# A hybrid diffusion block on one core: shift and scale of four K tiles as VectorE products, low halves of the sweep weights on GpSimd

## The chip, the cores and the metric

The kernel runs on one core of a Trainium2 chip. The metric is the device time of one execution in microseconds. The core has a matrix engine (TensorE, PE in the profile), a vector engine (VectorE, DVE), a scalar engine (ScalarE, ACT), GpSimd (POOL) and SyncE (SP), which in this kernel only issues transfers. A page of the profile gives times in us unless it marks them ns.

## The reference

The reference is one layer over 256 latent tokens and 256 context tokens, each with 2048 channels. Only the latent stream is returned. What matters for this change is the beginning:

```
sh1, sc1, g1, sh2, sc2, g2       = split(silu(c)     @ w_ada + b_ada, 6)    # latent tokens
sh1c, sc1c, ...                  = split(silu(c_ctx) @ w_ada + b_ada, 6)    # context tokens
h_l = rms_norm(x,   norm1_w) * (1 + sc1)  + sh1
h_c = rms_norm(ctx, norm1_w) * (1 + sc1c) + sh1c
projections = h_l @ w_in, h_c @ w_in
```

So each of the 2048 channels needs a shift and a scale for the latent stream and another pair for the context stream. Each of these is a dot product of 2048 terms: a column of `w_ada` with silu(c) or with silu(c_ctx). After that come gated linear attention, differential attention, gates, output projections, and a gated feed-forward network with a convolution. They use the other four sixths of the conditioning (`g1, sh2, sc2, g2`), for the latent stream alone. All inputs are 32-bit floats.

## The kernel before

Activations are kept transposed: 16 tiles, one for each group of 128 channels (the K tiles), channels on the partitions, tokens along the free dimension. Products are taken in a rounded 32-bit format. Every operand is split in two for accuracy: a high half, a rounded copy made by ScalarE (`split`, line 206), and a low half, the difference, made by VectorE (line 213). Three products of halves replace one exact product. `hl`/`ll` and `hc`/`lc` are the high and low halves of the modulated latent and context tokens.

**The first stage** is the `with` block from line 363 to line 599. It normalises and modulates both streams and at the same time multiplies them with a first part of `w_in`, the sweep weights: 896 columns, accumulated over the 16 K tiles in seven PSUM banks. In the loop of line 580, one turn k multiplies tile k (`sweep_row` for the first 512 columns, four token groups; `sweep_col` for the other 384 columns, three groups) and prepares tile k + 1. Preparing a tile means:

- `ada_rows` (line 463): sixteen small matrix products with silu(c) and silu(c_ctx) as the stationary side (columns 0 and 1 of `ccol_s`, 32 columns each) and the conditioning weights `w_ad1` of this tile as the moving side, 256 columns, in full 32-bit precision, in four row groups of the bank `ab`. ScalarE copies the result to `row`.
- `ada_cols` (line 474): two transposes on TensorE bring the sums onto the partitions. VectorE adds the four groups (`both`, line 482) and makes scale and shift (`shsc`, lines 483 and 484).
- `stage` (line 487): VectorE multiplies x by scale and by the root `z` (line 496), ScalarE adds the shift and rounds to the high half (line 498), VectorE makes the low half (line 502); once for each stream.
- `sweep_splits` (line 507): the halves of the sweep weights of the tile, 512 and 384 columns wide.

The first two tiles are prepared ahead of the loop, among the sums of squares for the norms.

**The order.** Inside this stage nearly everything is pinned: `pinned`, `kept` and `ordered_dma` hold each engine to the order in which the lines are written. SP issues the transfers in that order, too: the two inputs, tiles 0 and 1, then in each turn (`load`, line 406) the sweep weights and the four quarters of `w_ad1` of tile k + 2. A tile of conditioning weights is 2 MB, four buffers of 4 KB per partition; there are `SLOTS` = 12 such buffers, and four buffers for sweep weights. Outside this stage, the order is chosen by a planner with its own estimate of durations and by priorities written in the code.

**The other conditioning** is done on VectorE, in all the stages after this one. `w_ada` lies transposed in memory, so that output channels are on the partitions, and `cb` holds silu(c) broadcast to all partitions. `ada_load` (line 347) loads half a row tile, 512 KB, and `ada_dot` (line 354) multiplies it by half of `cb` and sums it, in one instruction. There are 128 of these; `ada_next(n)` (line 673) is called with fractions that say how many become due at each point. Six of them are done early, in turns 4 to 9 of the first stage (`EARLY_ADA`).

Of the kernel before, what the change touches and what calls it, by code (L numbers as in the profile page):

```python
# [9 lines left out]
F32 = mybir.dt.float32  # L10
# [3 lines left out]
AF = mybir.ActivationFunctionType  # L14
# [4 lines left out]
P = 128  # L19
# [19 lines left out]
SWW = 32 + C0 + (NGK + 1) * P  # L39
UPS = 6  # L40
CONVS = 7
SLOTS = 12
EARLY_ADA = 4, 10
GATE_ADA = [0.25] * 4 + [0.5] * 16 + [1] * 12
NRM = [(0, 0)] * 2 + [(j, j + 1) for j in range(12)] + [(12, 14), (14, 16)]

# [28 lines left out]
def _lay_out(i):  # L75
# [3 lines left out]
    w_ada = np.asarray(i["w_ada"])[0]  # L79
    w_in = np.asarray(i["w_in"])[0]  # L80
    a["xl"], a["xc"] = [np.ascontiguousarray(v.T.reshape(KT, P, T).transpose(1, 0, 2)) for v in (x, ctx)]
    c2 = np.stack([np.asarray(i["c"])[0], np.asarray(i["c_ctx"])])
    a["ccol"] = np.ascontiguousarray(c2.reshape(2, KT, P).transpose(2, 1, 0))
    g1 = w_ada[:, :2 * D].reshape(KT, P, 2, KT, P)
    a["w_ad1"] = np.ascontiguousarray(g1.transpose(3, 1, 0, 2, 4).reshape(KT, P, 2 * D))
    a["w_ada"] = np.ascontiguousarray(w_ada[:, 2 * D:].T.reshape(64, P, D))
    sweep = list(range(GA, GA + 32)) + list(range(GV, GV + C0)) + list(range(GK, GK + NGK * P)) + list(range(DKO, DKO + P))
# [59 lines left out]
def layer_kernel(tc, I, out):  # L147
# [3 lines left out]
    with es:  # L151
# [46 lines left out]
            for step in [work.pop(0) for _ in range(len(work))]:  # L198
                step()

        def split(raw, n, lows=None):


            hi = st.tile([P, 512], F32R, tag="hi", bufs=4, name="whi")
            lo = st.tile([P, 512], F32R, tag="lo", bufs=4, name="wlo")
            copied[0] = S.copy(hi[:, :n], raw)  # L206
            if pin[0]:
                tc.keep_in_program_order(copied[0])
            splits[0] += 1
            e = G if splits[1] and splits[0] % splits[1] == 0 else V  # L210

            def low():
                i = e.tensor_tensor(lo[:, :n], raw, hi[:, :n].bitcast(F32), op=ALU.subtract)  # L213
                if pin[0]:
                    tc.keep_in_program_order(i)
                if e is V:
                    copied[1] = i

            if lows is None:
                low()  # L220
            else:
                lows.append(low)
            return hi, lo

        def fetch(src, n):
            raw = st.tile([P, 1024], F32, tag="raw", bufs=4, name="wraw")
            nc.sync.dma_start(raw[:, :n], src)
            return raw
# [6 lines left out]
        ENDED = "h0 l0 h1 l1 h2 l2 l3 h3".split()  # L235
        SHIFTED = "h0 h1 l0 h2 l1 h3 l2 l3".split()

        def col_tile(src, acts, b, orders=None):

            nk = src.shape[1]
            nq = nk // 4
            tied = orders is not None
            orders = orders or [TURN] * (nq - 1) + [ENDED]
            for k0 in range(0, nk, 8):
                kn = min(8, nk - k0)
                if k0:  # L250
                    flush()
                raw = fetch(src[:, k0:k0 + kn, :].rearrange("p a b -> p (a b)"), kn * P)
                for kk in range(0, kn, 4):
                    whi, wlo = split(raw[:, kk * P:(kk + 4) * P], 4 * P)
                    order = orders[(k0 + kk) // 4]
                    for which in order:
                        j = int(which[1])
                        k = k0 + kk + j
                        sl = slice(j * P, (j + 1) * P)
                        first, last = k == 0 and which == "h0", k >= nk - 4 and which == order[-1]  # L260
                        if which[0] == "h":
                            i = PE.matmul(b.rearrange("p (a b) -> p a b", a=2), whi[:, sl], acts[k], start=first, stop=last)  # L262
                        else:
                            i = PE.matmul(b[:, T:], wlo[:, sl], acts[k][:, 1, :], start=False, stop=last)  # L264
                        if tied:
                            if chain:
                                after(i, chain[0])
                            chain[:] = [i]
                    if k0 and not kk:
                        flush(latest)  # L270
# [71 lines left out]

        ada2 = cp.tile([P, 64, 2], F32, name="ada2")
        adav = cp.tile([P, 64], F32, name="adav")
        ada_at, ada_due, ada_raw, ada_pool = [0], [EARLY_ADA[1] - EARLY_ADA[0]], [], [st, 2]

        def ada_load():
            j, q = divmod(ada_at[0], 2)
# [14 lines left out]
        with tc.tile_pool(name="first", bufs=1) as p1:  # L363
# [18 lines left out]
                return X[s][k // 4][:, k % 4 * T:(k % 4 + 1) * T]  # L382

            ada, raws1 = {}, {}

            def load_ada(k):

                ada[k] = [p1.tile([P, 1024], F32, tag="ada", bufs=SLOTS, name="ada") for q in range(4)]
                for q in range(4):
                    ordered_dma(ada[k][q], I["w_ad1"][k, :, q * 1024:(q + 1) * 1024])  # L390
# [15 lines left out]
            def load(k):  # L406
                if k < KT:
                    load_sweep(k)
                    load_ada(k)
# [53 lines left out]
            def ada_rows(k):  # L463

                w = ada.pop(k)
                for kk in range(KT):
                    j = 32 * (kk % 4)
                    pinned(ab[j:j + 32, :T], ccol_s[:, kk, :], w[kk // 4][:, kk % 4 * T:(kk % 4 + 1) * T],
                           start=kk < 4, stop=kk >= KT - 4, tile_position=(0, j))
                row = p1.tile([P, T], F32, tag="row", bufs=2, name="row")  # L470
                kept(S.copy(row, ab[:, :T]))
                return row
# [34 lines left out]
            def sweep_splits(k, lows=None):  # L507
                n = 32 + C0
                raw = raws1.pop(k)
                return split(raw[:, :n], n, lows), split(raw[:, n:SWW], SWW - n, lows)  # L510

            def sweep_row(k, w, t):
                n = 32 + C0
# [56 lines left out]
            stage(0, m, (1,))  # L570
            row, lows = ada_rows(1), []
            load(2)
            nxt = sweep_splits(1, lows)
            sweep_row(0, ws[0], 2)
            m = ada_cols(1, row)
# [4 lines left out]
            for k in range(1, KT):  # L580
                ws = nxt
                more = k + 1 < KT
                early = EARLY_ADA[0] <= k < EARLY_ADA[1]
                if early:
                    ada_load()
                load(k + 2)
                if more:
                    nxt = sweep_splits(k + 1)
                for t in range(4):
                    if more and t == 2:  # L590
                        row = ada_rows(k + 1)
                    sweep_row(k, ws[0], t)
                if more:
                    stage(k + 1, ada_cols(k + 1, row))
                if early:
                    ada_dot()
                for g in range(3):
                    sweep_col(k, ws[1], g)
            pin[0] = False

        r2 = es.enter_context(ExitStack())
# [71 lines left out]
        def ada_next(n):  # L673

            ada_due[0] += n
            while ada_at[0] < min(128, int(ada_due[0])):
                if len(ada_raw) == ada_pool[1]:
                    ada_dot()
                ada_load()
# [16 lines left out]
        with tc.tile_pool(name="gla", bufs=1) as pg:  # L696
# [17 lines left out]
                    value_rows(banks, ws, CR, 0, KT - 1, emptied)  # L714

            def q_tile(p, bank=acc_bank):
                ada_next(1 if p else 0.5)
                b = bank("gq")
                col_tile(I["w_in"][4 - NGK + p], A, b)
                S.activation(qk[p][:, 0, :], b[:, :T], AF.Copy, scale=DK ** -0.5)  # L720
                V.scalar_tensor_tensor(qk[p][:, 0, :], b[:, T:], DK ** -0.5, qk[p][:, 0, :], op0=ALU.mult, op1=ALU.add)

            def k_tile(p):
                ada_next(1.125)
                qk[p] = pg.tile([P, 3, T], F32, tag="qk", bufs=2, name="qk")
                b = acc_bank("gk")
                col_tile2(I["w_in"][p - NGK], b)
                S.copy(qk[p][:, 1:3, :].rearrange("p a b -> p (a b)"), b)

            def col_tile2(src, b):  # L730

                for k0 in range(0, KT, 8):
                    if k0:
                        flush()
                    raw = fetch(src[:, k0:k0 + 8, :].rearrange("p a b -> p (a b)"), 1024)
                    for kk in range(8):
                        if kk % 4 == 0:
                            whi, wlo = split(raw[:, kk * P:(kk + 4) * P], 512)
                        k = k0 + kk
                        both_tile(b, k, whi, wlo, slice(kk % 4 * P, (kk % 4 + 1) * P), k == 0, k == KT - 1)  # L740
                        if k0 and kk == 3:
                            flush(latest)

            def dk_tile(h):
                ada_next(0.5 if h > 3 else 1.25)
                b = acc_bank("dk")
                col_tile2(I["w_in"][7 - NGK + h], b)
                dk_done(h, b)

            def gr_tile(h):  # L750
                ada_next(0.25)
                b = acc_bank("gr")
                col_tile(I["w_in"][23 - NGK + h], A, b)
                added(gr[h // 2][:, h % 2 * T:(h % 2 + 1) * T], b)

            def gla_pair(p):
# [611 lines left out]
```

## Time and profile before

| what | value |
|---|---|
| median of 3 runs | 1689.82 us (1688.46 to 1691.17) |
| the profiled execution, its own time | 1687.6 us |
| span of the profiled execution, first to last instruction | 1685.5 us |
| granted TensorE clock | 1.00 |
| TensorE, VectorE, ScalarE, GpSimd busy | 99%, 76%, 58%, 20% of the span |
| `ab` products in the first stage (line 468) | 512 records, 30.9 us |
| modulating products `x` (line 496) | 32, 14.1 us |
| low halves of sweep weights on VectorE in the first 140 us, 512 and 384 wide | 20 of 689 ns, 16 of 597 ns |
| early conditioning products (line 356) | 6 of 1220 ns |
| DMA, first 120 us | 405 to 414 GB/s in each 10 us after the first |

Busy time is the time from an instruction's beginning to its end. Matrix products overlap in the pipeline, so a busy TensorE need not be one at its peak. A matrix product in full 32-bit precision appears as two records. A row of the chain of waits has the start in us, the length in us, and what ran; a row in order of time has start, length, engine, line, operation, and in brackets how long the engine had been idle and what ended that. The chain follows the work that ended last, from the last instruction backwards: what is not in it did not set the end.

### The profile page before, as it was taken

Reading aid. Unit: us, or ns where it says so; the run is one execution under the profiler, and the core shown is the slowest. Engines: PE = TensorE matmul, PEld = TensorE weight load, DVE = VectorE, ACT = ScalarE, POOL = GpSimd, SP = SyncE. Lnnn points to the kernel's source line nnn. Section 1 sums busy time; section 2 is a strip of 40 time slices with the busy share of each in tenths; the row PEclk is TensorE's granted clock in tenths of the full one; section 3 lists DMA queues with packets and bytes.
Section 4 is the critical chain, followed back from the end, with each engine's and each line's share of the span. In section 5 each row is a group of like instructions: output and inputs, shape, how many; then the busy total and the mean of one; then the engine's idle time right before and its main releaser. Section 6 shows DMA issues by size and latency. Waiting matters only on the chain.

```text
span 1685.5 us, 28601 instructions
## 1 busy us (share of the span) xinstructions
PE 1665.7 (99%) x10108; PEld 1438.4 (85%) x10108; DVE 1274.8 (76%) x2441; ACT 977.9 (58%) x1980; POOL 334.8 (20%) x431
## 2 busy tenths in 40 slices
PE   7999999999999999999999999999999999999998
PEld 5779999998788888888888998888888888888887
DVE  5557865768787888788998797878888787755655
ACT  5334554756355777666665686666666666544443
POOL 0001313231310000001324200222222222684000
PEclk9999999999999999999999999999999999999999
DMA  9995642435554555687877566667777676676654
GB/s 384 408 398 187 211 154 92 138 113 188 200 188 151 178 192 191 204 296 269 270 266 253 181 201 217 227 229 236 240 235 237 226 239 213 206 220 210 215 196 142
DMA packets 110833, 370.84 MB, mean 220 GB/s; under 512 B 14433, under 2 KB 19553, under 8 KB 110689
## 3 DMA queue, kind: packets, MB, share of 16 engines
q1 hardware_dynamic: 102112, 362.51, 63.5%
q10 hardware_dynamic: 4032, 4.37, 0.8%
q0 software_dynamic: 4544, 2.14, 0.6%
q8 instruction: 79, 1.29, 0.3%
q14 instruction: 66, 0.53, 0.1%
HBM read 364.73 MB, written 2.10 MB: 218 GB/s over the span
## 4 chain that ended last, share of the span: by engine, by line
PE 94%; DVE 3%; ACT 1%; DMA 1%; issue 1%; POOL 0%; SPq 0%; DVEq 0%
PE down L1321 14%; PE upg L262 9%; PE upv L262 9%; PE gate L262 7%; PE sweep L368 5%; PE upv L264 5%; PE upg L264 5%; PE gate L264 4%; PE mix L262 4%; PE mix L264 2%; PE pgb L262 2%; PE pga L262 2%; PE dk L333 2%; PE dvb L278 2%; PE dvb L279 2%; PE dk L331 2%
## 5 line engine op out<-in xcount | busy, mean ns | idle before, releaser
L206 ACT CAST whi<-wraw 128x512 fp32r<-128x512 f32 (+2 forms) x1004 | 604.9, 608 | 378.5 <-DVE wlo L213 111.3
L213 DVE TENSOR_TENSOR wlo<-wraw,whi 128x512 fp32r<-128x512 f32 (+2 forms) x932 | 637.3, 693 | 212.2 <-ACT whi L206 200.3
L262 PE MATMUL upg<-a,whi 128*128 128x512 f32 x656 | 229.0, 392 | 0.0
L262 PE MATMUL upv<-a,whi 128*128 128x512 f32 x656 | 229.0, 391 | 0.0
L1321 PE MATMUL down<-whi,g 128*128 128x512 f32 x704 | 216.7, 389 | 0.0
L264 PE MATMUL upv<-a,wlo 128*128 128x256 f32 x656 | 182.8, 280 | 0.0
L264 PE MATMUL upg<-a,wlo 128*128 128x256 f32 x656 | 182.6, 280 | 0.0
L262 PE MATMUL gate<-a,whi 128*128 128x512 f32 x512 | 179.8, 397 | 0.0
L213 POOL TENSOR_TENSOR wlo<-wraw,whi 128x512 fp32r<-128x512 f32 x72 | 100.3, 1393 | 388.1 <-ACT whi L206 383.9
L356 DVE CUSTOM_DVE_ANT_0 araw<-araw,cb 128x1024 f32<-128x1024 f32 x128 | 160.6, 1256 | 9.9 <-DMA araw<-in_w_ada 9.9
L1321 PEld LDWEIGHTS down<-whi,g 128*128 128x128 f32 x704 | 132.1, 188 | 27.5
L262 PEld LDWEIGHTS upv<-a,whi 128*128 128x128 f32 x656 | 122.4, 187 | 26.6
L262 PEld LDWEIGHTS upg<-a,whi 128*128 128x128 f32 x656 | 122.4, 187 | 26.5
L264 PE MATMUL gate<-a,wlo 128*128 128x256 f32 x512 | 139.9, 284 | 0.0
L1321 PE MATMUL down<-wlo,g 128*128 128x512 f32 x352 | 137.0, 389 | 0.0
L264 PEld LDWEIGHTS upv<-a,wlo 128*128 128x128 f32 x656 | 123.9, 189 | 0.5
L264 PEld LDWEIGHTS upg<-a,wlo 128*128 128x128 f32 x656 | 123.9, 189 | 0.5
L262 PEld LDWEIGHTS gate<-a,whi 128*128 128x128 f32 x512 | 94.3, 188 | 19.6 <-issue 0.7
L264 PEld LDWEIGHTS gate<-a,wlo 128*128 128x128 f32 x512 | 96.4, 188 | 5.6 <-issue 1.8
L262 PE MATMUL mix<-a,whi 128*128 128x512 f32 x256 | 89.1, 397 | 0.0
L1321 PEld LDWEIGHTS down<-wlo,g 128*128 128x128 f32 x352 | 66.1, 188 | 13.7
L1294 POOL DMA_DIRECT2D row<-turned x128 | 69.3, 549 | 28.7 <-DVE turned L1290 16.9
(351 smaller groups left out, 3395.0 us busy)
## 6 DMA issues: line engine op xcount, KB each, us to landing
wraw<-in_w_up SPq DMA_DIRECT2D x164, 512.0 KB, 4.3
araw<-in_w_ada SPq DMA_DIRECT2D x128, 512.0 KB, 4.9
wraw<-in_w_down SPq DMA_DIRECT2D x88, 512.0 KB, 3.4
ada<-in_w_ad SPq DMA_DIRECT2D x64, 512.0 KB, 10.0
wraw<-in_w_gate SPq DMA_DIRECT2D x64, 512.0 KB, 3.8
wraw<-in_w_in SPq DMA_DIRECT2D x58, 512.0 KB, 4.1
wraw<-in_w_proj SPq DMA_DIRECT2D x32, 512.0 KB, 4.3
wraw<-in_w_out SPq DMA_DIRECT2D x32, 512.0 KB, 4.5
```

Of the source, the lines that this page charges most:

```text
L206: copied[0] = S.copy(hi[:, :n], raw)
L213: i = e.tensor_tensor(lo[:, :n], raw, hi[:, :n].bitcast(F32), op=ALU.subtract)
L262: i = PE.matmul(b.rearrange("p (a b) -> p a b", a=2), whi[:, sl], acts[k], start=first, stop=last)
L264: i = PE.matmul(b[:, T:], wlo[:, sl], acts[k][:, 1, :], start=False, stop=last)
L278: PE.matmul(o, lo[k][:, ts], whi[:, sl], start=False, stop=False)
L279: return PE.matmul(o, hi[k][:, ts], wlo[:, sl], start=False, stop=last)
L331: PE.matmul(o, whi[:, sl], hi[k], start=first and j == 0, stop=False)
L333: i = PE.matmul(o, wlo[:, sl], hi[k], start=False, stop=last and j == 1)
L356: i = V.tensor_tensor_reduce(raw, raw, cb[:, q * 1024:(q + 1) * 1024], 1.0, 0.0, op0=ALU.mult, op1=ALU.add, accum_out=ada2[:, j, q:q + 1])
L368: return kept(PE.matmul(*args, **kw))
L1294: nc.gpsimd.dma_start(to[32 * (q % 4):32 * (q % 4 + 1), :, 32 * p:32 * (p + 1)], turned[32 * p:32 * (p + 1), :, 32 * q:32 * (q + 1)])
L1321: i = PE.matmul(banks[h][t][n], g[:, a, ts], w[n][b], start=k == 0 and (a, b) == (1, 0), stop=k == FT - 1 and b == 1)
```

## The change

Tiles 6, 9, 12 and 15 (`DOT_TILES`) no longer go through `ada_rows` and `ada_cols`. Their conditioning weights are laid out transposed (`w_ad1t`), loaded as four halves of 512 KB each, and each half is multiplied and summed on VectorE twice: by the broadcast silu(c) in `cb`, and by the broadcast silu(c_ctx) in a new tile `cbc`. The 32 products are dealt over turns 2 to 13 by `DOTS`, two or three to a turn, placed after `sweep_splits`. `dotted` combines the sums with three small GpSimd instructions into the shift and scale. Such a tile is staged at the beginning of the turn before its own, not at its end.

`cbc` comes from one transfer that broadcasts `c_ctx` to all partitions, issued after tile 2 (`load_ctx_row`). Its silu is made by three ScalarE passes over each half and a GpSimd multiplication (`silu_steps`, two passes in each of turns 1 to 3).

GpSimd makes the low halves of the sweep weights from tile 2 on. `ada_rows` moves from behind two token groups of `sweep_row` to behind one, and `ada_cols` from behind the fourth group to before it. The six early conditioning products of turns 4 to 9 become four late ones, loaded in turns 12 to 14 (`LATE_ADA`); the following stage takes up the other two, and there some of the `ada_next` calls are divided, so that a part comes in the middle of a tile (`adas`). The buffers for conditioning weights go from 12 to 11, and the descriptor scratch for transfers is set to 8192 bytes.

```
-SLOTS = 12
-EARLY_ADA = 4, 10
+SLOTS = 11
+DOT_TILES = 6, 9, 12, 15
+DOTS = [0, 0, 3, 3, 3, 2, 3, 3, 2, 3, 3, 2, 3, 2]
+LATE_ADA = {12: 1, 13: 1, 14: 2}
...
-            e = G if splits[1] and splits[0] % splits[1] == 0 else V
+            e = low_engine or (G if splits[1] and splits[0] % splits[1] == 0 else V)
...
-        ada_at, ada_due, ada_raw, ada_pool = [0], [EARLY_ADA[1] - EARLY_ADA[0]], [], [st, 2]
+        ada_at, ada_due, ada_raw, ada_pool = [0], [sum(LATE_ADA.values())], [], [st, 2]
...
+            cbc = p1.tile([P, D], F32, name="cbc")
+            junk = p1.tile([P, 1024], F32, name="junk")
+            sums2 = p1.tile([P, len(DOT_TILES), 2, 2, 2], F32, name="sums2")
+            dots = [(0, *d) for d in ((0, 0, 0), (0, 1, 0), (1, 0, 0), (0, 0, 1), (1, 0, 1), (1, 1, 0), (0, 1, 1), (1, 1, 1))]
+            dots += [(n, u, q, t) for n in range(1, len(DOT_TILES)) for u in (0, 1) for q in (0, 1) for t in (0, 1)]
...
+            def load_halves(k):
+                for n, u, q, t in dots_of[k]:
+                    if (n, u, q) not in halves_at:
+                        h = halves_at[n, u, q] = p1.tile([P, 1024], F32, tag="ada", bufs=SLOTS, name="ada")
+                        ordered_dma(h, I["w_ad1t"][n, u, :, q * 1024:(q + 1) * 1024])
+
+            def run_dots(k):
+                for n, u, q, t in dots_of[k]:
+                    h = halves_at[n, u, q]
+                    kept(V.tensor_tensor_reduce(h if t else junk, h, (cb, cbc)[t][:, q * 1024:(q + 1) * 1024], 1.0, 0.0,
+                                                op0=ALU.mult, op1=ALU.add, accum_out=sums2[:, n, u, t, q:q + 1]))
+
+            def dotted(k):
+                n = DOT_TILES.index(k)
+                m = p1.tile([P, 2, 2], F32, tag="shsc", bufs=2, name="shsc")
+                d = sums2[:, n]
+                kept(G.tensor_tensor(d[:, :, :, 0], d[:, :, :, 0], d[:, :, :, 1], op=ALU.add))
+                kept(G.tensor_scalar(m[:, 1], d[:, 1, :, 0], b1[:, k:k + 1], nw1[:, k:k + 1], op0=ALU.add, op1=ALU.mult))
+                kept(G.tensor_scalar(m[:, 0], d[:, 0, :, 0], vcol("b_ada", k), None, op0=ALU.add))
+                return m
...
+            def load_ctx_row():
+                ordered_dma(cbc, I["c_ctx"].to_broadcast([P, D]))
+                for q in range(2):
+                    x = cbc[:, q * 1024:(q + 1) * 1024]
+                    t = p1.tile([P, 1024], F32, tag="ada", bufs=SLOTS, name="silu")
+                    silu_steps.extend([
+                        lambda x=x, t=t: kept(S.activation(t, x, AF.Exp, scale=-1.0)),
+                        lambda x=x, t=t: kept(S.activation(t, t, AF.Ln, bias=1.0)),
+                        lambda x=x, t=t: (kept(S.activation(t, t, AF.Exp, scale=-1.0)),
+                                          kept(G.tensor_tensor(x, x, t, op=ALU.mult)))])
...
+                e = G if k > 1 else None
+                return split(raw[:, :n], n, lows, e), split(raw[:, n:SWW], SWW - n, lows, e)
...
             for k in range(1, KT):
                 ws = nxt
                 more = k + 1 < KT
-                early = EARLY_ADA[0] <= k < EARLY_ADA[1]
-                if early:
+                turned = more and k + 1 not in DOT_TILES
+                load(k + 2)
+                if k + 1 < KT:
+                    load_halves(k + 1)
+                for _ in range(LATE_ADA.get(k, 0)):
                     ada_load()
-                load(k + 2)
+                if more and not turned:
+                    stage(k + 1, m)
                 if more:
                     nxt = sweep_splits(k + 1)
+                run_dots(k)
+                if k + 2 in DOT_TILES:
+                    m = dotted(k + 2)
                 for t in range(4):
-                    if more and t == 2:
+                    if turned and t == 1:
                         row = ada_rows(k + 1)
+                        for step in silu_steps[:2]:
+                            step()
+                        del silu_steps[:2]
+                    if turned and t == 3:
+                        cols = ada_cols(k + 1, row)
                     sweep_row(k, ws[0], t)
-                if more:
-                    stage(k + 1, ada_cols(k + 1, row))
-                if early:
-                    ada_dot()
+                if turned:
+                    stage(k + 1, cols)
                 for g in range(3):
                     sweep_col(k, ws[1], g)
+                for _ in range(LATE_ADA.get(k - 1, 0)):
+                    ada_dot()
...
             def q_tile(p, bank=acc_bank):
-                ada_next(1 if p else 0.5)
+                ada_next(0.5)
                 b = bank("gq")
-                col_tile(I["w_in"][4 - NGK + p], A, b)
+                col_tile(I["w_in"][4 - NGK + p], A, b, adas=0.5 if p else 0)
...
-    nc = _bacc.Bacc("TRN2", target_bir_lowering=False, num_devices=1)
+    nc = _bacc.Bacc("TRN2", target_bir_lowering=False, num_devices=1,
+                    dynamic_dma_scratch_size=8192)
```

More of the change, by code (lines that the diff above doesn't have):

```diff
@@ L81, in _lay_out @@
     a["xl"], a["xc"] = [np.ascontiguousarray(v.T.reshape(KT, P, T).transpose(1, 0, 2)) for v in (x, ctx)]
+    a["c_ctx"] = np.ascontiguousarray(np.asarray(i["c_ctx"])[None])
     c2 = np.stack([np.asarray(i["c"])[0], np.asarray(i["c_ctx"])])
@@ L84, in _lay_out @@
     g1 = w_ada[:, :2 * D].reshape(KT, P, 2, KT, P)
+    a["w_ad1t"] = np.ascontiguousarray(w_ada[:, :2 * D].reshape(D, 2, KT, P)[:, :, list(DOT_TILES)].transpose(2, 1, 3, 0))
     a["w_ad1"] = np.ascontiguousarray(g1.transpose(3, 1, 0, 2, 4).reshape(KT, P, 2 * D))
@@ L199, in flush, with split @@
                 step()
-        def split(raw, n, lows=None):
+        def split(raw, n, lows=None, low_engine=None):
             hi = st.tile([P, 512], F32R, tag="hi", bufs=4, name="whi")
@@ L236, in layer_kernel, with col_tile @@
         SHIFTED = "h0 h1 l0 h2 l1 h3 l2 l3".split()
-        def col_tile(src, acts, b, orders=None):
+        def col_tile(src, acts, b, orders=None, adas=0):
             nk = src.shape[1]
@@ L252, in col_tile @@
                 raw = fetch(src[:, k0:k0 + kn, :].rearrange("p a b -> p (a b)"), kn * P)
+                if k0 and adas:
+                    ada_next(adas)
                 for kk in range(0, kn, 4):
@@ L384, in layer_kernel @@
             ada, raws1 = {}, {}
+            cbc = p1.tile([P, D], F32, name="cbc")
[3 more added lines that the diff above has]
+            dots += [(n, u, q, t) for n in range(1, len(DOT_TILES)) for u in (0, 1) for q in (0, 1) for t in (0, 1)]
+            dots_of, at = [], 0
+            for n in DOTS + [0] * KT:
+                dots_of.append(dots[at:at + n])
+                at += n
@@ new lines, in layer_kernel @@
+            assert at == len(dots)
+            halves_at = {}
+            def load_halves(k):
[8 more added lines that the diff above has]
+                                                op0=ALU.mult, op1=ALU.add, accum_out=sums2[:, n, u, t, q:q + 1]))
@@ new lines, in layer_kernel @@
+            silu_steps = []
+            def load_ctx_row():
[8 more added lines that the diff above has]
+                                          kept(G.tensor_tensor(x, x, t, op=ALU.mult)))])
@@ L386, in load_ada @@
             def load_ada(k):
+                if k in DOT_TILES:
+                    return
                 ada[k] = [p1.tile([P, 1024], F32, tag="ada", bufs=SLOTS, name="ada") for q in range(4)]
@@ L509, in sweep_splits @@
                 raw = raws1.pop(k)
-                return split(raw[:, :n], n, lows), split(raw[:, n:SWW], SWW - n, lows)
+                e = G if k > 1 else None
+                return split(raw[:, :n], n, lows, e), split(raw[:, n:SWW], SWW - n, lows, e)
             def sweep_row(k, w, t):
@@ L572, in layer_kernel @@
             load(2)
+            load_ctx_row()
             nxt = sweep_splits(1, lows)
@@ L723, in k_tile, with col_tile2 @@
             def k_tile(p):
-                ada_next(1.125)
+                ada_next(1)
                 qk[p] = pg.tile([P, 3, T], F32, tag="qk", bufs=2, name="qk")
                 b = acc_bank("gk")
-                col_tile2(I["w_in"][p - NGK], b)
+                col_tile2(I["w_in"][p - NGK], b, 0.5)
                 S.copy(qk[p][:, 1:3, :].rearrange("p a b -> p (a b)"), b)
-            def col_tile2(src, b):
+            def col_tile2(src, b, adas=0):
                 for k0 in range(0, KT, 8):
@@ L735, in col_tile2 @@
                     raw = fetch(src[:, k0:k0 + 8, :].rearrange("p a b -> p (a b)"), 1024)
+                    if k0 and adas:
+                        ada_next(adas)
                     for kk in range(8):
@@ L744, in dk_tile @@
             def dk_tile(h):
-                ada_next(0.5 if h > 3 else 1.25)
+                ada_next(0.5 if h > 3 else 0.75)
                 b = acc_bank("dk")
-                col_tile2(I["w_in"][7 - NGK + h], b)
+                col_tile2(I["w_in"][7 - NGK + h], b, 0 if h > 3 else 0.75)
                 dk_done(h, b)
@@ L752, in gr_tile @@
                 b = acc_bank("gr")
-                col_tile(I["w_in"][23 - NGK + h], A, b)
+                col_tile(I["w_in"][23 - NGK + h], A, b, adas=0 if h else 0.5)
                 added(gr[h // 2][:, h % 2 * T:(h % 2 + 1) * T], b)
```

## The prediction

> **What bounds the kernel now.** I first read the page's span and busy times, then the chain of waits through the first stage, then the stage in windows.
>
> ```profile
> span 1685.5 us, 28601 instructions
> PE 1665.7 (99%) x10108; PEld 1438.4 (85%) x10108; DVE 1274.8 (76%) x2441; ACT 977.9 (58%) x1980; POOL 334.8 (20%) x431
> ```
>
> ```profile
> 37.53 3.54 PE sweep L368 x24
> 41.07 1.86 PE ab L368 x32
> 42.94 1.58 PE sweep L368 x6
> 44.52 0.22 PE ab L480 x2
> 44.74 3.52 PE sweep L368 x24
> ```
>
> TensorE is idle for only 20 us of the whole span. In the chain, one turn of the K loop is 1.58 + 0.22 + 3.52 + 1.86 = 7.2 us, with nothing but TensorE in it. Of that, the conditioning (`ab`, lines 468 and 480) takes 1.86 + 0.22 = 2.08 us. The turn for k = 2 begins at about 39.5 us (row 37.53: its first eighteen matmuls, some 2 us, belong to the turn before), so the turn for k begins at 39.5 + 7.2 (k - 2).
>
> ```profile
> 0.00:10.00 10.00, 3.63 (x17) 3.66 (x18) 2.95 (x8) 6.34 (x10) 0.98 (x6) 1.00 0.84 302
> 10.00:20.00 10.00, 8.60 (x63) 6.16 (x63) 5.18 (x13) 5.69 (x13) 0.00 (x0) 1.00 1.03 414
> 20.00:30.00 10.00, 8.88 (x71) 6.37 (x70) 5.85 (x12) 5.70 (x13) 0.00 (x0) 1.00 1.03 408
> 90.00:100.00 10.00, 10.00 (x99) 7.19 (x101) 7.22 (x17) 3.14 (x8) 0.00 (x0) 1.00 1.03 407
> ...
> ada<-in_w_ad SPq DMA_DIRECT2D x64, 512.0 KB, 10.0
> wraw<-in_w_sw SPq DMA_DIRECT2D x15, 448.0 KB, 9.9
> ```
>
> The last two numbers of a window are the DMA share and GB/s. The transfers run without a break at about 408 GB/s beside the busy TensorE: the stage has two near-equal limits. The granted clock is 1.00 throughout, so it drops out.
>
> **When a tile arrives.** By 30 us, 3.02 + 4.14 + 4.08 = 11.24 MB have moved. In queue order the last quarter of conditioning tile 2 stands at 12.0 MB: 20 transfers of 0.524 MB, three of 0.459 and 0.17 of small ones. It is moved at about 31.9 us. When it has landed:
>
> ```profile
> 31.44 0.33 SPq L340 DMA_DIRECT2D wraw<-in_w_sw  x1
> 32.70 4.01 SPq L340 DMA_DIRECT2D ada<-in_w_ad  x4
> ```
>
> 10.0 us to landing at 408 GB/s are eight transfers in flight, and SP issues one each time the eighth ahead has landed. The second of these four, at about 34.0, follows that quarter. So a transfer lands 2 us after its bytes have moved: landing = 32 + (M - 11.24)/0.408 us, M its place in MB.
>
> **The change, its gain.** Four turns (k = 5, 8, 11, 14) lose 2.08 us of TensorE each and become 5.1 us: 8.3 us in all, if nothing else binds.
>
> **Its cost in transfers, early.** The broadcast context row, 1.05 MB, goes in front of tile 3, and three halves of transposed weights, 1.57 MB, between tiles 3 and 4. The last quarter of tile 3 moves from M = 14.6 to 15.64 and lands at 42.8, the third half (17.21) at 46.6. VectorE's three products of turn k = 2 stand ahead of tile 3's `both`, `shsc` and `x` in its written order, so their delay is TensorE's. Durations on VectorE:
>
> ```profile
> 88.05 0.17 DVE L482 TENSOR_REDUCE both<-ab 128x4 f32<-128x16 f32 x1 [2.51 <-PE ab L480]
> ...
> 88.58 0.87 DVE L496 SCALAR_TENSOR_TENSOR x<-x,shsc,z 128x256 f32<-128x256 f32 x2
> 89.10 0.51 ACT L498 ACTIVATE a<-x,shsc 128x256 fp32r<-128x256 f32 x1 [2.46 <-DVE x L496]
> ...
> 89.64 0.48 DVE L502 SCALAR_TENSOR_TENSOR a<-x,shsc,a 128x256 fp32r<-128x256 f32 x1 [0.18 <-ACT a L498]
> ...
> 90.04 0.48 DVE L502 SCALAR_TENSOR_TENSOR c<-x,shsc,c 128x256 fp32r<-128x256 f32 x1
> 90.44 1.22 DVE L356 CUSTOM_DVE_ANT_0 araw<-araw,cb 128x1024 f32<-128x1024 f32 x1
> ...
> 91.59 1.15 DVE L213 TENSOR_TENSOR wlo<-wraw,whi 128x512 fp32r<-128x512 f32 x2
> ```
>
> A product takes 1.15 us to the next instruction (90.44 to 91.59). From `both` to `x` is 0.53, from `x` to the end of ScalarE's high half 1.03 (88.58 to 89.61): a tail of 1.56. Two `lo` products follow, the engine being free 0.83 after that high half. At the least, then, turn 3 begins at 46.6 + 1.15 + 1.56 = 49.3 instead of 46.7. Then tile 4 (its last quarter now at 19.77 MB) lands at 52.9; from that quarter's matmuls to the turn's end are 5.1 us (0.46 + three row groups 2.4 + transposes 0.22 + columns 2.0), so turn 4 begins no earlier than 58.0. Tile 5 (22.85 MB) lands at 60.5, so turn 5 no earlier than 65.6, against 61.1 before: **+4.5 us**, forced by bytes alone. From tile 7 on the transfers keep up: turns 5 to 7 ask for 7.7 MB, 18.8 us at 408 GB/s, in TensorE's 5.1 + 2 x 7.2 = 19.5 us. SP's count hardly changes: sixteen quarter loads become sixteen halves of the same 512 KB, one context row is new, and of the six early loads of turns 4 to 9 four remain, in turns 12 to 14, behind all that the stage still needs except tile 15's sweep weights.
>
> **Its cost on GpSimd and VectorE.** The low halves leave VectorE (1.15 us a turn, last row above) for GpSimd. What they do to VectorE there is seen in a later stage, where the same low half runs on GpSimd, in a list of VectorE and GpSimd instructions in order of time:
>
> ```profile
> 1102.80 1.22 DVE L356 CUSTOM_DVE_ANT_0 araw<-araw,cb 128x1024 f32<-128x1024 f32 x1
> 1103.64 1.53 POOL L213 TENSOR_TENSOR wlo<-wraw,whi 128x512 fp32r<-128x512 f32 x1 [4.25 <-ACT whi L206]
> 1103.95 0.08 DVE L356 DVE_READ_ACCUMULATOR2_ANT ada<- 128x1 f32 x1
> 1103.95 1.51 DVE L232 TENSOR_TENSOR g<-C,g 128x256 fp32r<-128x256 f32 x1
> ...
> 1124.99 0.42 DVE L232 TENSOR_TENSOR g<-C,g 128x256 fp32r<-128x256 f32 x1
> 1125.82 1.29 POOL L213 TENSOR_TENSOR wlo<-wraw,whi 128x512 fp32r<-128x512 f32 x1 [4.25 <-ACT whi L206]
> 1126.05 0.42 DVE L274 TENSOR_TENSOR C<-upg,C 128x256 f32<-128x256 f32 x1 [0.64 <-ACT C L273]
> ```
>
> Alone, the low half takes 1.29 us and a VectorE sum of two SBUF tiles 0.42. When they meet, GpSimd waits for the running product to end, and then VectorE's next instruction lasts 1.51: it lost 1.09 us. An instruction that reads PSUM (L274) loses nothing. So a 512 low half takes 1.09 us out of VectorE's two-tile work, a 384 one about 0.82 (three quarters), 1.91 a turn against 1.15 before. Nearly all of VectorE's work here (products, `x`, `lo`) has two SBUF inputs; only `both` and the `shsc` pair, 0.53 us, can run beside GpSimd.
>
> The Trainium skill's page "SBUF — State Buffer", section "SBUF: two separate sides", calls this an exclusive lock: whichever begins first holds the shared pair for the whole instruction, and the other blocks fully. By that rule nothing is shared out at all; the 1.51 agrees. What it would make of the time is the first rival below.
>
> A turned turn with three products, if all of it queues up: 0.83 + 3 x 1.15 + 1.91 + 1.56 = 7.75 us between high halves, against TensorE's 7.2. A short turn followed by a turned one: 0.83 + 1.87 (both `x`, ScalarE, both `lo` of the next tile) + 2 x 1.15 + 1.91, then 3 x 1.15 + 1.91 + 1.56, in all 13.8, against TensorE's 12.3. If the second low half of each turn falls wholly under the 0.53 of `both` and `shsc`, each turn is shorter by that. I take half, 0.25 a turn, since VectorE's order decides it and the row shows a full block.
>
> - Turns 5 to 7: 13.3 + 7.5 = 20.8 against 21.6: -0.8. The same for 8 to 10.
> - Turns 11 to 13 (the last with two products only, so 7.2): 20.5, -1.1.
> - Turn 14, short and without products: -2.1.
>
> The context row's silu falls in turns 2 and 3: ScalarE's six passes are off the path, about 1.0 us each by doubling this row and taking off its fixed part, but GpSimd's two 1024-wide multiplications hold VectorE for twice 1.09 each.
>
> ```profile
> L437 ACT ACTIVATE sq<-x 128x512 f32<-128x512 f32 x14 | 7.5, 615 | 0.0
> L1143 POOL TENSOR_TENSOR raw<-adav,raw 128x2 fp32r<-128x2 f32 x16 | 4.6, 310 | 0.0
> ```
>
> With these and all low halves in the way, turn 2: first half at 44.0, product to 45.2, GpSimd to 47.4, two products to 49.7, tail to 51.2 (+4.5); turn 3: 7.75 + 2.18 = 9.9 (+7.2); turn 4: +0.55, **+7.8** at turn 5. Between 4.5 and 7.8 I take the middle, 6.1. The three small GpSimd instructions per product tile (310 ns row, some 1.2 us) have most of a turn before VectorE's `x` wants them: nothing; without that cover, 1.2 us four times.
>
> **Sum: 6.1 - 0.8 - 0.8 - 1.1 - 2.1 = +1.3 us.**
>
> Costed at nothing: the two loads and products moved behind the stage, the others cut in two, and the smaller descriptor scratch.
>
> ```profile
> PE dk L333 <- DVE wlo L213: 2.0, 2, 1.7
> ...
> 1480.00:1520.00 40.00, 40.00 (x178) 33.14 (x177) 21.86 (x34) 18.09 (x29) 30.97 (x58) 1.00 0.74 218
> ```
>
> Two more products are 2.3 us of VectorE in a stage where TensorE rarely waits for it; bounds: +2.3 if they hit such a wait, -2.0 if the new places remove this one. GpSimd's transfers run where TensorE is busy 40.00 of 40.00 us; a smaller ring there would first eat that cover. At the stage's end SP holds a late load for a product of turn 13 or 14, and the next stage's first weights queue behind it; they have the 5.1 us of turn 15 as cover.
>
> **Rivals.** First, full blocking: every low half and both silu multiplications take their whole time out of VectorE in the chain, so VectorE with GpSimd is the bound from turn 2 to 12. 7.8 + 0 + 0 - 0.6 - 2.1 = +5.1, **slower**: 1694.9. It decides as soon as the hidden part is under about 0.1 us a turn. For it speaks the 1.51; against it that low halves have a whole turn to run. Had the low halves stayed on VectorE, 1.15 would stand for 1.91. Second, no blocking on the path: GpSimd slips into the time in which VectorE waits for transposes or transfers, TensorE binds from turn 5: 4.5 - 8.3 = -3.8, 1686.0, and up to 2 us lower with the wait at `dk`. Against it: with three products VectorE has almost no such time. Third, the context row, one 8 KB row read for 128 partitions, moves slowly, or a half waits for one of eleven buffers: at half the rate 2.6 us more at turn 2, about +3.9, 1693.7. No row shows such a source.
>
> **How the numbers follow.** The profiled execution took 1687.6 us (span 1685.5 and 2.1 around it), 2.2 under the median of the runs, 1689.8; I add the sum to the median: 1691.1. Chances: forecast 0.48, full blocking 0.24, no blocking 0.20, slow row 0.08. The range 1684.8 to 1695.4 holds both main rivals. What can be told from no change is 0.2%, 3.4 us (under 1686.4, over 1693.2). No blocking is mostly faster; full blocking mostly slower, with half of the slow row and a tail of the forecast: faster 0.22, same 0.48, slower 0.30. The forecast's own range is 1688 to 1694.
>
> **What would show it.** `ab` matmuls fall from 512 records to 384. Turn 5 begins at 65 to 69 us instead of 61.1, with TensorE idle in turns 2 to 4. GpSimd's low halves last over 1.29 us, or VectorE instructions with two SBUF inputs show 1.0 us too much behind them; turned turns of 7.2 would show no blocking, 7.7 full. The stage's last turn begins about where it did, near 133 us. The forecast is wrong if turn 5 begins before 65, if TensorE does not idle in turns 6, 7, 9 and 10, or if the time arises after the stage.

## The result and the profile after

The changed kernel takes 1695.72 us in the median (1694.63 to 1696.74) where the kernel before takes 1689.14: a ratio of 1.0038, interval 1.0025 to 1.0051. It is slower by 6.6 us. The forecast was 1691.1, its range ended at 1695.4; the first rival, full blocking, had said 1694.9.

The page of the changed kernel and who kept TensorE waiting in its first 200 us (columns: us in total, times, longest):

```profile
span 1693.5 us, 28384 instructions
PE 1661.9 (98%) x9972; PEld 1435.7 (85%) x9972; DVE 1318.4 (78%) x2465; ACT 985.5 (58%) x1982; POOL 406.4 (24%) x473
```

```profile
PE sweep L374 <- ACT a L552: 11.0, 9, 3.3
PE sweep L374 <- DMA ident<-in_ident: 6.5, 1, 6.5
PE hss L683 <- DVE wlo L217: 0.8, 1, 0.8
PE sweep L374 <- ACT c L552: 0.7, 1, 0.7
PE gaT L975 <- DVE g L974: 0.7, 2, 0.4
```

TensorE has less to do (1661.9 us against 1665.7), and a longer span. The new row is the first: nine times it waits for the high half of a tile, 11 us in all. Before, this row stood at 0.9 us, a single wait within the first 30 us. A high half comes from ScalarE, but ScalarE itself waits for VectorE's `x`. When each turn could begin is read from the end of the latent high half. Here are those of turns 4, 5, 7, 8 and 10, after (the tiles of turns 6 and 9 are staged ahead), and, in the second fence, of turns 5 and 7 before:

```profile
60.46 0.51 ACT L552 ACTIVATE a<-x,shsc 128x256 fp32r<-128x256 f32 x1 [3.62 <-DVE x L550]
...
68.17 0.51 ACT L552 ACTIVATE a<-x,shsc 128x256 fp32r<-128x256 f32 x1 [3.82 <-DVE x L550]
...
82.01 0.51 ACT L552 ACTIVATE a<-x,shsc 128x256 fp32r<-128x256 f32 x1 [5.03 <-DVE x L550]
...
89.74 0.51 ACT L552 ACTIVATE a<-x,shsc 128x256 fp32r<-128x256 f32 x1 [3.85 <-DVE x L550]
...
103.58 0.51 ACT L552 ACTIVATE a<-x,shsc 128x256 fp32r<-128x256 f32 x1 [5.03 <-DVE x L550]
```

```profile
60.30 0.51 ACT L498 ACTIVATE a<-x,shsc 128x256 fp32r<-128x256 f32 x1 [2.46 <-DVE x L496]
...
74.70 0.51 ACT L498 ACTIVATE a<-x,shsc 128x256 fp32r<-128x256 f32 x1 [2.46 <-DVE x L496]
```

Turn 5 begins 7.9 us late (68.17 against 60.30). From there a short and a turned turn together take 13.84 us (68.17 to 82.01, 89.74 to 103.58), a turned one with three products 7.7 (60.46 to 68.17, 82.01 to 89.74). Before, the pairs took 14.4 and single turns 7.2. Why they take so long is seen on VectorE and GpSimd in turns 5 and 6, in order of time:

```profile
71.44 1.22 DVE L412 CUSTOM_DVE_ANT_0 ada<-ada,cbc 128x1024 f32<-128x1024 f32 x1
71.60 8.36 POOL L217 TENSOR_TENSOR wlo<-wraw,whi 128x512 fp32r<-128x512 f32 x4 [3.30 <-ACT whi L210]
...
72.59 2.30 DVE L412 CUSTOM_DVE_ANT_0 junk<-ada,cb 128x1024 f32<-128x1024 f32 x1
...
74.93 1.90 DVE L412 CUSTOM_DVE_ANT_0 ada<-ada,cbc 128x1024 f32<-128x1024 f32 x1
...
76.77 2.31 DVE L412 CUSTOM_DVE_ANT_0 junk<-ada,cb 128x1024 f32<-128x1024 f32 x1
```

The first product takes its 1.22. Then GpSimd runs four low halves back to back and between any two of them VectorE gets one product: 2.30 behind a 512-wide low half, 1.90 behind a 384-wide one. That is 1.08 and 0.68 more than the product needs, and nothing of it is hidden. (In the other turns of the stage it is 2.17 to 2.31 and 1.90 to 2.03.) Over the first 145 us, by groups:

```profile
L412 DVE CUSTOM_DVE_ANT_0 junk<-ada,cb 128x1024 f32<-128x1024 f32 x16 | 31.2, 1952 | 4.2 <-DMA ada<-in_w_ad1t 4.0
L217 POOL TENSOR_TENSOR wlo<-wraw,whi 128x512 fp32r<-128x512 f32 x14 | 29.8, 2130 | 59.9 <-ACT whi L210 55.8 <-DVE c L556 4.1
L412 DVE CUSTOM_DVE_ANT_0 ada<-ada,cbc 128x1024 f32<-128x1024 f32 x16 | 28.5, 1792 | 0.3
L217 POOL TENSOR_TENSOR wlo<-wraw,whi 128x384 fp32r<-128x384 f32 x14 | 24.9, 1781 | 0.0
```

32 products last 59.7 us; at 1.22 each they would last 39.0.

Where the 6.6 us arose can be followed by the same matmuls in both traces. The last one of `gq`, with which the first stage is done, starts at 143.44 before and 148.39 after: +4.95. The first of the next group, `gvb`, starts at 144.37 and 151.88: +7.5, so 2.5 more are lost within four microseconds. From there to the end of the two profiled executions 0.5 is added, what is left of losses and a gain: the last matmul of `gvb` starts 8.8 us later than before, as the granted clock has fallen meanwhile (last section), the last of `z` (384.2 us before) 6.9 later, the last of `down` 8.0. The two executions lie 8.0 us apart, the medians 6.6.

### The profile page after: what moved, and what is told of

Its sections match the earlier page's. It is cut to its first block, busy times and chain, and to the rows that moved or that the text cites. A ratio compares the mean times of both kernels' runs of the same rounds, so it can differ in the third digit from the quotient of the medians.

```text
span 1693.5 us, 28384 instructions
## 1 busy us (share of the span) xinstructions
PE 1661.9 (98%) x9972; PEld 1435.7 (85%) x9972; DVE 1318.4 (78%) x2465; ACT 985.5 (58%) x1982; POOL 406.4 (24%) x473
## 4 chain that ended last, share of the span: by engine, by line
PE 89%; DMA 5%; DVE 4%; issue 1%; ACT 0%; POOL 0%; SPq 0%; DVEq 0%; ACTq 0%
PE down L1391 14%; PE upg L268 9%; PE upv L268 9%; PE gate L268 7%; PE upv L270 5%; PE upg L270 5%; PE gate L270 4%; PE mix L268 4%; DMA ada<-in_w_ad 2%; DMA wraw<-in_w_sw 2%; PE mix L270 2%; PE pgb L268 2%; PE pga L268 2%; PE dk L339 2%; PE dk L338 2%; PE dk L337 2%
## 5 line engine op out<-in xcount | busy, mean ns | idle before, releaser
L217 DVE TENSOR_TENSOR wlo<-wraw,whi 128x512 fp32r<-128x512 f32 (+2 forms) x904 | 622.1, 696 | 218.0 <-ACT whi L210 205.0
L217 POOL TENSOR_TENSOR wlo<-wraw,whi 128x512 fp32r<-128x512 f32 x100 | 154.5, 1551 | 448.0 <-ACT whi L210 435.3
L1191 POOL TENSOR_TENSOR C<-pt,C 128x256 f32<-128x256 f32 x16 | 29.9, 1869 | 197.1 <-DVE pt L280 197.1
```

Of the source, the lines that this page charges most:

```text
L1191: (G if j > c else V).tensor_tensor(gates[j], t, gates[j], op=ALU.mult)
```

## Experiments

**Low halves back on VectorE.**

```
-                e = G if k > 1 else None
+                e = None
```

> Edit: the changed kernel, but the low halves of the sweep weights stay on VectorE; the products, the context row and all else as changed. Theory 1 (full blocking: a low half on GpSimd takes 1.09 and 0.82 us out of VectorE, on VectorE itself only 1.15 together): a turned turn with three products is 0.83 + 3.45 + 1.15 + 1.56 = 7.0 us, a short and a turned one together 12.3, so TensorE (7.2 and 12.3) sets the turns from 4 on; turn 5 begins 6.5 us later than before the change instead of 7.6, the four short turns then win 8.3 back, and the first stage ends 1 to 2 us earlier than before the change: about 1688 to 1690, 6 us under the changed kernel. Theory 2 (VectorE is simply too full, whoever makes the low halves): the 1.15 us come back on VectorE in each of 14 turns, so the time is that of the changed kernel or longer, 1696 to 1703. Theory 3 (the early transfers alone cost the time): unchanged, 1695 to 1696.

Measured: 1687.78 us beside 1689.39 of the kernel before, ratio 0.9988 (0.9980 to 0.9997). One line takes 8 us off the changed kernel and makes it a little faster than the kernel before, just below the expected range. From turn 5 on a pair takes 12.4 us and a single turn 7.15, as TensorE alone would have it. The products, over the first 140 us:

```profile
L412 DVE CUSTOM_DVE_ANT_0 junk<-ada,cb 128x1024 f32<-128x1024 f32 x16 | 21.5, 1342 | 3.4 <-DMA ada<-in_w_ad1t 3.4
L412 DVE CUSTOM_DVE_ANT_0 ada<-ada,cbc 128x1024 f32<-128x1024 f32 x16 | 19.4, 1220 | 0.2
```

The context products are back at 1220 ns. Theories 2 and 3 are out. But turn 5 began 8.9 us later than before the change (69.20 against 60.30, in an execution whose first high half came 0.9 earlier), not 6.5. Two things in turn 3 account for it:

```profile
59.41 2.44 POOL L436 TENSOR_TENSOR cbc<-cbc,silu 128x1024 f32<-128x1024 f32 x1 [11.67 <-ACT silu L435]
59.50 3.04 DVE L550 SCALAR_TENSOR_TENSOR x<-x,shsc,z 128x256 f32<-128x256 f32 x2
```

```profile
48.00:50.00 2.00, 0.28 (x3) 0.07 (x1) 1.97 (x3) 0.00 (x0) 0.00 (x0) 1.00 1.03 410
50.00:52.00 2.00, 0.38 (x1) 0.38 (x2) 1.78 (x8) 0.94 (x3) 0.00 (x0) 0.60 1.02 408
52.00:54.00 2.00, 2.00 (x11) 0.86 (x14) 1.98 (x5) 0.89 (x2) 0.00 (x0) 0.50 1.04 414
54.00:56.00 2.00, 2.00 (x24) 0.99 (x20) 2.00 (x5) 0.00 (x0) 0.00 (x0) 0.50 1.03 380
56.00:58.00 2.00, 2.00 (x12) 1.07 (x5) 1.11 (x2) 1.09 (x2) 0.00 (x0) 0.69 0.99 385
```

The second silu multiplication on GpSimd fell on `x` itself: 3.04 us for a pair that takes 0.88. And the granted TensorE clock (the third number from the end in a window) fell to 0.60, 0.50, 0.50 and 0.69, after TensorE had waited 3.35 us for tile 3's high half: the `ab` matmuls of that turn lasted 3.6 us instead of 1.9. In the changed kernel the same wait is 3.33 us long, and the clock stayed at 1.00. SP waited for buffers, too:

```profile
SPq L346 <- PE ab L374: 5.9, 3, 5.1
...
SPq L346 <- POOL cbc L436: 2.6, 1, 2.6
```

The two temporaries of the silu sit among the eleven buffers of the conditioning weights until that multiplication, and tile 5's quarters were issued over 8.7 us instead of 4 (SP's waits are from 36 to 62 us). But no loss from that shows: the `ab` matmuls of turn 4, which read these quarters, ran in 1.93 us without a wait.

**Without the context row.**

```
-            load_ctx_row()
...
-  ... (cb, cbc)[t][:, q * 1024:(q + 1) * 1024] ...
+  ... cb[:, q * 1024:(q + 1) * 1024] ...
```

> Edit: the changed kernel without the broadcast context row, its silu passes and its two GpSimd multiplications; the products for the context stream of the four tiles take the latent row instead (so their context shift and scale are left out, and the latent ones stand in their place). Number and size of products, halves and low halves are unchanged. By the sum of transfers and blocking, turn 5 then begins about 2 us later than before the change instead of 7.6, the turns behind it stay at 13.8 and 7.7: 5 to 6 us under the changed kernel, about 1690. If the early loss came from the three halves and products alone, little changes: 1694 to 1696.

Measured: 1689.64 us, ratio 1.0000 (0.9990 to 1.0009): 6.1 under the changed kernel. The high half of turn 5 ends at 62.73 us against 60.81 before the change: 1.9 late, where 2 were expected. The pairs behind it take 13.8 us and the single turns 7.7, as in the changed kernel. So the row, with what hangs on it, is worth 6 of the 7.9 us that the early turns lose.

**Only the low halves on GpSimd, in the kernel before.**

```
+                e = G if k > 1 else None
-                return split(raw[:, :n], n, lows), split(raw[:, n:SWW], SWW - n, lows)
+                return split(raw[:, :n], n, lows, e), split(raw[:, n:SWW], SWW - n, lows, e)
```

> Edit: the kernel before, with nothing changed but that GpSimd makes the low halves of the sweep weights from tile 2 on. Theory 1 (blocking costs only where VectorE is full): VectorE has 3 us free in each turn of 7.2, the high half still comes before TensorE asks for it: within 1 us of the kernel before, 1688 to 1691. Theory 2 (each low half on GpSimd costs the path by itself, 0.76 us more than on VectorE in 14 turns): 10 us slower, about 1700.

Measured: 1688.84 us, ratio 0.9997 (0.9988 to 1.0006): no difference. The turns are 7.2 us throughout. VectorE's wait for the transposed conditioning, over the first 140 us, shows the room it has (43.0 us in the kernel before, for `PE ab`):

```profile
L482 DVE TENSOR_REDUCE both<-ab 128x4 f32<-128x16 f32 x16 | 2.8, 174 | 60.1 <-PE ab L480 59.5 <-ACT whi L206 0.6
```

```profile
L213 POOL TENSOR_TENSOR wlo<-wraw,whi 128x512 fp32r<-128x512 f32 x14 | 24.1, 1721 | 82.0 <-ACT whi L206 77.4 <-DVE c L502 4.6
L213 POOL TENSOR_TENSOR wlo<-wraw,whi 128x384 fp32r<-128x384 f32 x14 | 14.0, 1003 | 0.0
```

The same 28 low halves whose move to GpSimd makes 8 us in the changed kernel cost this one nothing that can be measured. The blocking is a price only where VectorE's two-input work fills the turn, and it is the products that fill it.

**Only what lies behind the first stage.** The first stage of the kernel before with `EARLY_ADA = 4, 8`; the divided `ada_next` calls and the descriptor scratch of 8192 bytes as changed.

> Edit: the first stage of the kernel before (with four early conditioning products instead of six), and of the change only what lies behind that stage: the divided and redistributed loads, two more of them there, and the descriptor scratch of 8192 bytes. The prediction costed this at nothing: within 1 us of the kernel before, 1688 to 1690.5. If the 1.6 us by which the measured loss exceeds the sum for full blocking lie in this part, it is 1690.5 to 1692.

Measured: 1687.58 us, ratio 0.9988 (0.9980 to 0.9997): 1.8 faster, with 0.5 to 3.4 in the interval. This part of the change is not the missing loss; the time lies below both expected ranges. The wait of TensorE at `dk`, 2.0 us in the row that the prediction shows, is down to 0.3; a wait at `sc` has grown (200 to 700 us of the profile, first this kernel, then the kernel before):

```profile
PE sc L840 <- DVE e L872: 1.5, 2, 1.0
...
PE dk L340 <- DVE wlo L218: 0.3, 1, 0.3
```

```profile
PE sc L831 <- DVE e L863: 0.2, 1, 0.2
```

The two profiled executions end only 0.3 us apart (spans 1685.2 and 1685.5), so the traces show less of a gain than the medians.

**Silu by ScalarE's own function, the low halves still on GpSimd.**

```
-                        lambda ...: kept(S.activation(t, x, AF.Exp, scale=-1.0)),
-                        lambda ...: kept(S.activation(t, t, AF.Ln, bias=1.0)),
-                        lambda ...: (kept(S.activation(t, t, AF.Exp, scale=-1.0)),
-                                     kept(G.tensor_tensor(x, x, t, op=ALU.mult)))
+                silu_steps.extend([table("silu_and_others"), silu_of(0), silu_of(1),
+                                   table("natural_log_exp_and_others")])
```

> Edit: the changed kernel, with the silu of the broadcast context row made by ScalarE's Silu itself (two passes and two loads of an activation table in turns 1 and 2) in place of six passes and two GpSimd multiplications. The transfers, the products and the low halves on GpSimd stay. If the two multiplications take 2.18 us each out of VectorE, turn 3 begins at 49.3 instead of 51.2, turn 4 at 58.0 (bound by tile 4's transfers), turn 5 at about 65.8 to 66 instead of 68.7, and the turns behind stay at 13.8 and 7.7: about 3 us under the changed kernel, 1692 to 1693.5. If they cost nothing, 1695 to 1696.

Measured: 1691.85 us beside 1688.57 of the kernel before, ratio 1.0019 (1.0010 to 1.0028): 3.9 under the changed kernel, or 3.3 if each is taken beside the kernel before of its own set of runs (+3.3 and +6.6). The high half of turn 3 ends at 49.45 (51.40 in the changed kernel), that of turn 5 at 64.87 (68.68), and the turns behind stay at 13.8 and 7.7. The second product of turn 2, in the changed kernel first and in this one second, in order of time:

```profile
44.93 2.63 POOL L436 TENSOR_TENSOR cbc<-cbc,silu 128x1024 f32<-128x1024 f32 x1 [2.60 <-ACT silu L435]
...
45.45 3.20 DVE L412 CUSTOM_DVE_ANT_0 junk<-ada,cb 128x1024 f32<-128x1024 f32 x1
```

```profile
45.47 1.23 DVE L412 CUSTOM_DVE_ANT_0 junk<-ada,cb 128x1024 f32<-128x1024 f32 x1 [0.16 <-DMA ada<-in_w_ad1t]
```

The half landed at the same time in both; behind the multiplication its product took 1.97 us more.

**Both mended: low halves on VectorE, silu by table.** With four tiles as changed; with tiles 9, 12 and 15 and the context row behind tile 6; with tiles 12 and 15 and the row behind tile 7.

```
-DOT_TILES = 6, 9, 12, 15
-DOTS = [0, 0, 3, 3, 3, 2, 3, 3, 2, 3, 3, 2, 3, 2]
+DOT_TILES = 9, 12, 15
+DOTS = [0] * 5 + [2, 3, 3, 2, 3, 3, 2, 3, 3]      # or: 12, 15 with
+                                                  # [0] * 6 + [1, 2, 2, 2, 1, 2, 3, 3]
...
+                if k == CTX_AT:                   # 4, or 5
+                    load_ctx_row()
```

> Edit: both together, the low halves of the sweep weights on VectorE and the silu by table; four tiles, transfers as changed. Blocking gone, only the early transfers are left: turn 5 begins 4.5 us late, then TensorE sets 12.3 and 7.2 a turn and the four short turns give 8.3 back; with the 1.8 us that the later stages gave by themselves, 3.8 + 1.8 under the kernel before: 1683 to 1686. If the blocking is not what the early turns lose, it stays where the low halves alone brought it, 1687 to 1688.

> Edit: as the four-tile kernel with low halves on VectorE and silu by table, but only tiles 9, 12 and 15 by products (24, in turns 5 to 13), and the context row loaded in turn 4, behind tile 6. The early loss falls to what tiles 7 and 8 arrive late, 1.5 to 2 us; three short turns give 6.2 back: 4 to 5 us plus the 1.8 of the later stages, 1682 to 1685. If early transfers are not a limit, it loses against the four-tile kernel: about 2 us slower than it.

> Edit: the same with tiles 12 and 15 alone (16 products, one to three a turn in turns 6 to 13, one new half a turn), the context row behind tile 7. No transfer comes late by the byte count, so the two short turns give all of 4.2 back: with the 1.8 of the later stages 1683 to 1684.5. If the products themselves cost the path something where VectorE has room, it is nearer to 1687.

Measured beside 1688.57 of the kernel before: four tiles 1683.04, ratio 0.9965 (0.9952 to 0.9977); three 1683.00, 0.9965 (0.9953 to 0.9977); two 1682.92, 0.9962 (0.9950 to 0.9975). All three beat both kernels, by 5.5 to 5.7 us and by some 12 us, and cannot be told apart. What TensorE still waits for from 30 to 200 us, in the three in that order:

```profile
PE ab L374 <- DMA ada<-in_w_ad: 1.5, 2, 0.9
PE sweep L374 <- ACT a L553: 1.4, 1, 1.4
```

```profile
PE sweep L375 <- ACT a L554: 1.3, 1, 1.3
PE ab L375 <- DMA ada<-in_w_ad: 0.7, 1, 0.7
```

```profile
PE gvb L286 <- DVE wlo L218: 0.5, 1, 0.5
PE ab L375 <- DMA ada<-in_w_ad: 0.4, 1, 0.4
```

The fewer tiles go by products, the less TensorE saves (8.3, 6.2, 4.2 us) and the less it loses to early transfers. The three-tile kernel was expected to win on the four-tile one and did not, nor did it lose. Its high half of turn 7 ends 9.9 us after that of turn 6 instead of 7.2; TensorE waited 2.0 us there (the two rows), and 1.5 to 2 had been counted.

## Why the prediction was wrong

- **What bounds the kernel, the rates and the arrivals** were right. The first product of turn 2 waited for its half and began at 44.07, where 44.0 had been computed. The second half, by the same rate due at 45.4, let its product begin at 45.47 where nothing else held it (silu by table).
- **The gain** was right: short turns win about 2.0 us each (2.08 predicted) as soon as nothing blocks, 12.4 us a pair and 7.15 a turn with the low halves on VectorE.
- **The price of a low half** was nearly right: 0.95 to 1.09 us for 512 columns (1.09 predicted), 0.68 to 0.81 for 384 (0.82 predicted). In turns 5 and 6, from start to start of the products (72.59, 74.93, 76.77), the two together take 1.88 us out of VectorE (1.91 predicted). A silu multiplication took 1.97 (2.18 predicted).
- **The step that failed is "I take half, 0.25 a turn"**, and with it "between 4.5 and 7.8 I take the middle, 6.1". Nothing was hidden. The full sums of the prediction came out within 0.2 us: a turned turn 7.7 (7.75), a short and a turned one 13.84 (13.8), turn 3 at 51.4 (51.2), turn 4 at 61.0 (61.1), turn 5 at 68.7 (68.9). The stage ended 4.95 late; the first rival had said 5.1. So this step is 3.8 of the 5.3 us by which the forecast of +1.3 missed the measured +6.6. Of turn 5's delay the silu multiplications make over 3 us (68.68 against 64.87 with the table, of which 0.6 is an earlier first high half); the rest stands with the low halves on VectorE as well (64.88 in the four-tile kernel). The 0.53 us of `both` and `shsc` do not read two SBUF tiles, but they stand behind the last product of the turn in VectorE's order, and GpSimd, which asks as soon as ScalarE has cast, had by then taken its turns between the products. The middle between two bounds was a choice without a mechanism, though the one row that showed the collision showed no sharing.
- The Trainium skill's rule ("SBUF — State Buffer", "SBUF: two separate sides": whoever begins first holds the pair for the whole instruction, the other blocks fully) agrees with this: every product behind a 512-wide low half took 2.17 to 2.31 us. It should have been the forecast and not its rival. A sentence of the same page of the Trainium skill, section "Who interferes with whom", that a two-input instruction on VectorE contends with a GpSimd instruction that reads SBUF, covers the products, `x` and `lo`; the runs show it for the products and, in turn 3 of the kernel with low halves on VectorE, for `x`.
- **"Costed at nothing"** failed in one place and was on the safe side in another. The edits in the later stages cost nothing by themselves: the medians show a gain of 1.8 us (bound -2.0), while in the traces the wait at `dk`, 1.7 shorter, is mostly made up for by the one at `sc`, 1.3 longer. The passage from the first stage to the next loses 2.5 in the changed kernel. The prediction had looked there at SP's queue alone and found cover; what TensorE waits for is VectorE, which copies two `sweep` banks before it makes the low halves that `hss` and `gvb` need; in the kernel before it makes them first. The experiments without the context row and with silu by table have the same order and the same 1.5 us of idle TensorE between 140 and 160 us; the four- and three-tile kernels with low halves on VectorE have none (the two-tile one 0.5). Low halves on GpSimd alone do not bring it, since the kernel before with that one edit has none either. Why the order changes stays open; no run isolates it. Nor do the runs show how the last microsecond or two between trace and median are shared out.
- **The third rival** is not borne out. The first half behind the context row landed when the full rate said. SP did wait for one of the eleven buffers, 4.0 us within tile 5's quarters in the changed kernel, but the `ab` matmuls of turn 4 that read them ran in 1.93 us without a wait.

What the experiments make of the 6.6 us, each beside the kernel before of its own set of runs: without the low halves on GpSimd +6.6 becomes -1.6, a difference of 8.2; without the silu multiplications +3.3, a difference of 3.3; without both -5.5, a difference of 12.1. The 8.2 are not the blocking in the turns alone: from turn 5's high half to that of turn 14 the changed kernel takes 63.4 us (68.17 to 131.59) and the one with low halves on VectorE 58.0 (69.20 to 127.19), 5.4 less; the passage behind the stage makes up most of the rest. With both edits, what is left is the TensorE gain of 8.3 less an early transfer loss of about 4 (turn 5 at 64.88 against 60.81): the first `gvb` matmul of the four-tile kernel starts at 140.19, 4.2 us earlier than before the change. The rest, 1.3 us, comes from the later stages.

## What to carry to other kernels

Before work is moved to an engine with time to spare, ask what it takes from the engine that has none: GpSimd was 20% busy here, but each of its low halves took most of its own length (some 1.1 of 1.29 us for 512 columns) out of VectorE's two-input work. The same move costs nothing while VectorE has room, and becomes the bound with the next change that fills VectorE; so count both engines as one queue in the stage where they meet. When a row of the trace shows a full block, let the full sum be the forecast and ask for a named reason before taking anything off it.

## What the runs showed of the hardware

That GpSimd, with four instructions waiting, and VectorE take turns strictly, one instruction each, so that a GpSimd low half of 1.29 us lasts 2.13 in the mean and both are slowed, was more regular than expected. And the granted TensorE clock fell behind the first stage of the changed kernel, in windows of 2 us:

```profile
150.00:152.00 2.00, 0.99 (x4) 0.72 (x5) 2.00 (x6) 1.41 (x4) 0.00 (x0) 1.00 0.04 9
152.00:154.00 2.00, 2.00 (x13) 2.00 (x12) 1.94 (x5) 1.89 (x4) 0.00 (x0) 0.59 0.46 102
154.00:156.00 2.00, 2.00 (x11) 2.00 (x11) 1.89 (x5) 0.29 (x2) 0.00 (x0) 0.56 0.51 176
156.00:158.00 2.00, 2.00 (x18) 2.00 (x17) 0.87 (x3) 0.39 (x1) 1.43 (x2) 1.00 0.00 0
```

It is 0.59 and 0.56 from 152 to 156 us, which is some 1.7 us of full clock, after 150 to 152 in which TensorE was busy for half of the time, with no idle piece over 0.85 us. The kernel with silu by table shows the same fall (0.50 and 0.72 from 148 to 152 us, behind 2 us in which TensorE was busy for 0.85). The kernel without the context row has the same pieces of idle time in the same place at a clock of 1.00. A wait of over 3 us in turn 2 was followed by 1.00 in the changed kernel (3.33 us) and by 0.60 and 0.50 in the one with low halves on VectorE (3.35 us). The Trainium skill's page "TensorE: Matmul & The Clock Gate", Part 1, gives half the clock after an idle window of about 3.4 us. The fall behind 3.35 us agrees with that. The other falls agree in depth, not in this condition: the idle pieces before them were 0.85 us at most. No run here shows what set those off.

Such falls are not in every execution. Between 450 and 470 us the profiled executions with low halves on VectorE, without the context row, and with only the low halves on GpSimd have one window of 10 us at 0.83; those of the other kernels have 1.00 there. In the last of the three, which had started `dvb` 0.1 us behind the kernel before, `gate` starts 3.3 us behind it. So a difference of 2 or 3 us between two single traces need not come from the edit.
